# A hybrid decoder trunk on one core: the last merge on DVE, four banks for late projections, a deferred contraction block, taps behind inputs, and a shorter turn of the state space groups

## The chip, the cores and the metric

The kernel runs on one core of a Trainium2 chip. The core has a matrix engine (TensorE, PE in the profile), three engines for elementwise work (VectorE or DVE, ScalarE or ACT, GpSimd or POOL) and SyncE (SP), whose queue issues all DMAs of this kernel. The metric is device time in microseconds of one launch. Before the change it is 1704.26 us, the median of 3 runs (1700.07 to 1706.83).

## The reference

The input is one sequence of 1024 tokens of width 1024, and there are two layers. Each normalizes, mixes, normalizes the result and adds it to its input:

```python
for i in range(DEPTH):                      # DEPTH = 2
    if i % 2 == 0:
        h = rms_norm(x, attn_pre_norm)
        h = dilated_attention_mixer(h, w_in, w_out, rel_bias)
        x = x + rms_norm(h, attn_post_norm)
    else:
        h = rms_norm(x, ssm_pre_norm)
        h = s5_mixer(h, ...)
        x = x + rms_norm(h, ssm_post_norm)
```

The attention mixer projects to queries, keys and values of three groups (16 heads of 64, windows 128, 512 and 2048 with dilations 1, 4 and 16) and to a gate z. Each group gives an output and a log-sum-exp. The three outputs are merged by a softmax over the log-sum-exps, multiplied by silu(z), and projected by `w_out`:

```python
wts = softmax(stack(lses), axis=0)
o = sum(wts[..., None] * stack(outs), axis=0)
return (o * silu(z)) @ w_out
```

The state space mixer projects to u and z, runs 64 groups of 16 channels with 64 complex diagonal states over time, and gates twice:

```python
y = s5_scan(u, ...)                         # states x_t = a x_{t-1} + b u_t,  y = Re(C x) + d u
g = gelu(y)
y = g * sigmoid(g @ w_glu + b_glu)
return (y * silu(z)) @ w_out
```

## The kernel before

All matrix products take fp32 operands as a high and a low part, so each is three matmuls (high by high, high by low, low by high). Splitting a tile is a cast on ACT (L83) and a subtraction on DVE or POOL (L84), in `split`. A projection of 128 output columns is done in two halves of 512 tokens (`th` 0 and 1); a half is `proj_half`: one PSUM bank and 8 x 3 matmuls with 512 columns (L110). PSUM has eight banks, in pools of two: `psj` for projections, `pst` for transposes, `pso`, and `psl` or `psa`. The bank of a half comes free when ACT and DVE have read it.

The order of the instructions on each engine is fixed when the program is built: a planner goes by program order, by estimated times and by priorities (`high_priority(AHEAD)` moves a block ahead in program order). At run time each engine takes its instructions strictly in that order, and so does SP with its DMA issues. `issue_after(ins)` keeps the instructions of a block behind `ins` on that engine.

The stages that the change touches, in time:

1. **Attention, last pair.** Eight pairs of heads (`attn_pair`) give outputs O[0] to O[2], 128 x 1024 each, in four rotating buffers of tag `O`. `merge_weights` computes the softmax of the log-sum-exps and stores it to DRAM (`wt_dr`); `weights_of` loads it back, spread over the partitions; `merge` (L679) multiplies the three outputs by their weights and adds them up. For pairs 4 to 7 it also multiplies by the gate, which was computed early and lies in `g_dr`. The merge of pair p runs during pair p + 1 on POOL. That of the last pair (p = 7) runs at L832: products on DVE (L684, L690), the two sums on POOL (L686), with the `wraw` buffers for the weights.
2. **Gate projections** (`attn_gate`, L795). The gates of pairs 0 to 3 are projected here: eight halves through `in_order`. For each, `use` (L815) takes the silu of the bank (`silu2`: ACT L791, DVE L792), loads the pair's merged output from `on_dr`, multiplies on POOL (L822) and splits it into `gh` and `gl` (L825). `early(p)` loads and splits the finished pairs 4 to 7. The raw weights `w_out` come through `load_out` (L803).
3. **Output projection** (`attn_out`, `out_tiles`, L894). The split `w_out` (`woh`, `wol`, L938) goes to the buffers of the normalized activations (`a0` to `a3`). The first four banks, (i, n) = (0,0), (1,0), (0,1), (1,1), run over the contraction blocks k (one for each pair) at L846 to L848. With `late=0` they run over all eight before any other tile; with `late` they leave out block 7, and do it for the four banks afterwards.
4. **Layer 1** (`layer1`, L1382). Sixteen projections of two halves, eight for u and eight for z, go through `in_order` with `start="half"`, which treats the first two projections apart. After half t `run(t)` issues what the list `at` has for t: for each of eight state space groups `ssm_loads` (tables BT, Cg, Sg and CA), `ssm_taps` (eight DMAs of 64 KB, L1318), `ssm_input` (U, written by `use_u` as `u_dr`), `ssm_states` (matmuls L1339, then a chain on DVE and POOL to X) and `ssm_outputs` (matmuls L1366 and L1367, the gelu on ACT, POOL and DVE, and the store to `y_dr`). A group follows the one before by three halves. The taps of groups 0 to 3 and of 4 to 7 lie in the buffers `b1` and `b3`. `use_z` evicts a z half on ACT (L1396) and DVE (L1397).
5. **GLU** (`glu`, L1421). It loads y back (`gy`, L1431), splits it into g, whose first half (`g0b`) lies in `b1` and `b3`, and starts with four open banks, the last contraction block at the end.

The GLU's later projections and the second output projection follow, untouched.

Of the kernel before, what the change touches and what calls it, by code (L numbers as in the profile page):

```python
# [15 lines left out]
F32 = mybir.dt.float32  # L16
# [7 lines left out]
P = 128  # L24
# [89 lines left out]
def proj_half(c, w, h):  # L114

    ps = c.psj.tile([P, H], F32, tag="psj", name="psj")
    proj_part(c, ps, w, h, range(KT))
    return ps
# [504 lines left out]
def big(c, p, name):  # L623

    if p == 7:
        return c.wraw.tile([P, S], F32, tag="wraw", name=name)
    return c.attn.tile([P, S], F32, tag="mw", name=name, bufs=2)


def weights_of(c, p, g):  # L630

    w = big(c, p, "mw")
    off = c.wt_dr.offset + (p * 3 + g) * 2048
    for h in range(2):
        c.nc.sync.dma_start(w[HEADS[h]], bass.AP(c.wt_dr.tensor, off + h * S, [[0, 64], [1, S]]))
    return w


def attn_pair(c, p, w_in, h):
# [28 lines left out]
    if p == 7:  # L668
        merge_weights(c, p)
    c.merge = lambda: merge(c, p, O)  # L670
# [8 lines left out]
def merge(c, p, O):  # L679

    nc = c.nc
    for g in range(3):
        engine = nc.vector if p == 7 else nc.gpsimd
        engine.tensor_tensor(O[g], O[g], weights_of(c, p, g), op=ALU.mult)  # L684
    for g in range(2):
        nc.gpsimd.tensor_tensor(O[2], O[2], O[g], op=ALU.add)  # L686
    if p >= EARLY:
        w = big(c, p, "mg")
        nc.sync.dma_start(w, c.g_dr[p])
        (nc.vector if p == 7 else nc.gpsimd).tensor_tensor(O[2], O[2], w, op=ALU.mult)  # L690
    if p == 7:
        c.last = O[2]
    else:
        nc.sync.dma_start(c.on_dr[p], O[2])
# [54 lines left out]
def in_order(c, srcs, h, use, after=None, start=None, ws=()):  # L749
# [21 lines left out]
    elif start == "half":  # L771
        for e in range(2):
            one(e, 0, proj_half(c, ws[e], h[0]))
        pss = [c.psj.tile([P, H], F32, tag="psj", name="psj") for _ in range(2)]
        for part in range(2):
            cs = slice(part * 256, part * 256 + 256)
            for e in range(2):
                proj_part(c, pss[e][:, cs], ws[e], [x[:, :, cs] for x in h[1]], range(KT), part == 0)
                if part:
                    one(e, 1, pss[e])  # L780
    for e in range(len(ws), len(srcs)):
        w = load_w(c, srcs[e])
        for th in range(2):
            one(e, th, proj_half(c, w, h[th]))

# [9 lines left out]
def attn_gate(c, a, h):  # L795
# [9 lines left out]
    def early(p):  # L805
        load_out(p, 0)
        for i in range(2):
            if p == 7:
                f = c.last[:, i * H:i * H + H]
            else:  # L810
                f = c.slot("fz")
                nc.sync.dma_start(f, c.on_dr[p, :, i * H:i * H + H])
# [13 lines left out]

    def step(t):
        if t < 7 - EARLY:
            early(EARLY + t)

    in_order(c, [a["w_in"][48 + p] for p in range(EARLY)], h, use, step)
    run_merge(c)  # L832
# [95 lines left out]
def attn_out(c, a, g, raw):  # L928
# [28 lines left out]
    out_tiles(c, g, w, post, lambda i: xv[i], done)  # L957
# [332 lines left out]
def ssm_loads(self):  # L1290
# [8 lines left out]
    self.CA = tl("CA", 144)  # L1299
# [7 lines left out]
    nc.sync.dma_start(self.CA, c.ca_dr[et].rearrange("p (g x) -> p g x", g=8))  # L1307


def ssm_taps(self):  # L1310
# [5 lines left out]
    for m in range(8):  # L1316
        src = bass.AP(c.k_dr.tensor, c.k_dr.offset + et * 8 * 16 * 240 + 16 * m, [[240, 16], [16 * 240, 8], [1, 128]])
        c.nc.sync.dma_start(t[16 * m:16 * m + 16], src)  # L1318


def ssm_input(self):
    c = self.c
    self.U = c.ssm.tile([P, 8, P], F32, name="U", tag="U", bufs=2)
    c.nc.sync.dma_start(self.U, c.u_dr[self.et].rearrange("p (g n) -> p g n", g=8))
# [57 lines left out]
def layer1(c, a, h1, ws):  # L1382
# [20 lines left out]
    for e in range(8):  # L1403
        t = 3 * e
        for stage, d in ((ssm_loads, (-1, -2)[e] if e < 2 else 3), (ssm_taps, 4), (ssm_input, 5), (ssm_states, 7), (ssm_outputs, 10)):
            at[t + d + 1].append((stage, e))

    def run(t):
        for stage, e in at[t + 1]:
            stage(groups[e])  # L1410
# [40 lines left out]
def trunk(tc, a):  # L1451
# [3 lines left out]
    c.turn = 0  # L1455
    with ExitStack() as es:
# [160 lines left out]
```

## Time and profile before

| what | value |
|---|---|
| median of 3 runs | 1704.26 us (1700.07 to 1706.83) |
| the profiled execution | 1699.39 us |
| its span, first to last instruction | 1697.6 us |
| mean granted TensorE clock | 0.992 |
| matmuls (PE) | 9714 |
| DMA | 212.19 MB, mean 125 GB/s |
| HBM read, written | 153.51 MB, 56.96 MB |

A row of a group or of the timeline names the line of the kernel, the engine, the operation and the tiles, written before read (out<-in); x3 means three instructions. In the timeline the first two numbers are start and duration in us, and the brackets tell how long the engine sat idle before and what ended that. A row of a stretch gives its two ends and its length, then the busy time of PE, weight load (PEld), DVE, ACT and POOL, then the granted clock of TensorE as a share of full speed, the mean busy share of the DMA engines and GB/s. A row of a wait reads "who waits <- for whom: us in total, times, longest". All times in the rows count from the start of the span. SPq is SP issuing a DMA: its duration is that of the issue, not of the transfer.

### The profile page before, as it was taken

How to read it: one execution, taken by the hardware profiler on the slowest of the kernel's cores; microseconds unless marked ns; L12 is line 12 of the kernel's file. 1: busy time of each engine (PE TensorE's matmuls, PEld its weight loads, DVE VectorE, ACT ScalarE, POOL GpSimd, SP SyncE). 2: the span in 40 equal slices, each digit the busy share in tenths (PEclk: the TensorE clock that was granted, in tenths of full speed). 3: DMA queues.
4: the chain of work that ended last, by engine and by line, in shares of the span. 5: the costliest groups of instructions: out<-in, count | busy, mean ns of one | idle time of the engine just before them, and what ended most of it. 6: DMA issues, size and time to landing. Idle time of an engine off the chain costs nothing. (4 is left out here: it accounts for less than half of the span.)

```text
span 1697.6 us, 26292 instructions
## 1 busy us (share of the span) xinstructions
PE 1657.5 (98%) x9714; PEld 1397.0 (82%) x9714; DVE 1014.2 (60%) x2509; ACT 711.9 (42%) x1730; POOL 461.0 (27%) x303
## 2 busy tenths in 40 slices
PE   8999999999999999999999999999999999989998
PEld 6889999978888888888888888877887888867886
DVE  8698898625554554545454554657562787755533
ACT  5232232236465464655555454653452223233411
POOL 2000001132242525223351614213220445413121
PEclk9999999999999999999999999999999999989999
DMA  6223455532331423232242424236259865465432
GB/s 236 84 55 101 147 175 162 174 95 65 87 106 54 117 70 103 78 91 90 77 117 82 113 68 124 78 110 167 87 169 237 232 203 202 143 186 162 149 118 87
DMA packets 176857, 212.19 MB, mean 125 GB/s; under 512 B 37443, under 2 KB 133462, under 8 KB 176728
## 3 DMA queue, kind: packets, MB, share of 16 engines
q1 hardware_dynamic: 176728, 210.52, 41.5%
q8 instruction: 76, 1.25, 0.3%
q14 instruction: 53, 0.43, 0.1%
HBM read 153.51 MB, written 56.96 MB: 124 GB/s over the span
## 5 line engine op out<-in xcount | busy, mean ns | idle before, releaser
L110 PE MATMUL psj<-hh,whi 128*128 128x512 f32 x896 | 359.6, 401 | 3.7 <-DVE tz L792 3.7
L110 PE MATMUL psj<-hh,wlo 128*128 128x512 f32 x896 | 359.4, 401 | 0.0
L110 PE MATMUL psj<-hl,whi 128*128 128x512 f32 x896 | 356.4, 398 | 0.0
L84 POOL TENSOR_TENSOR wlo<-wraw,whi 128x1024 fp32r<-128x1024 f32 x48 | 115.2, 2400 | 395.4 <-ACT whi L83 365.1
L110 PEld LDWEIGHTS psj<-hh,whi 128*128 128x128 f32 x896 | 169.6, 189 | 41.2 <-DVE tz L792 4.1
L110 PEld LDWEIGHTS psj<-hh,wlo 128*128 128x128 f32 x896 | 169.4, 189 | 36.6
L110 PEld LDWEIGHTS psj<-hl,whi 128*128 128x128 f32 x896 | 169.4, 189 | 36.4
L486 ACT ACTIVATE lg<-lg,nm 128x128 f32<-128x128 f32 (+1 forms) x384 | 168.2, 442 | 37.4 <-DVE nm L481 37.4
L83 ACT CAST whi<-wraw 128x1024 fp32r<-128x1024 f32 x80 | 83.7, 1046 | 192.5 <-PE psj L110 127.1
L475 DVE CUSTOM_DVE_ANT_0 lg<-psl,T 128x128 f32<-128x128 f32 (+1 forms) x384 | 110.6, 347 | 88.6 <-PE psl L469 88.6
L371 PE MATMUL psq<-whi,v 128*128 128x256 f32 x640 | 120.3, 284 | 0.0
L110 PE MATMUL psj<-h1h,whi 128*128 128x512 f32 (+1 forms) x272 | 106.7, 393 | 8.0 <-DVE z L1397 7.8
L84 DVE TENSOR_TENSOR ph<-pt,ph 128x512 fp32r<-128x512 f32 (+2 forms) x160 | 96.8, 622 | 15.3 <-ACT ph L83 13.1
L110 PE MATMUL psj<-h1l,whi 128*128 128x512 f32 (+1 forms) x272 | 105.7, 389 | 0.1
L110 PE MATMUL psj<-h1h,wlo 128*128 128x512 f32 (+1 forms) x272 | 105.2, 388 | 0.0
L84 DVE TENSOR_TENSOR kl<-psj,kh 128x512 fp32r<-128x512 f32 x48 | 33.2, 692 | 119.8 <-ACT kh L83 119.2
L371 PEld LDWEIGHTS psq<-whi,v 128*128 128x128 f32 x640 | 100.0, 189 | 1.2 <-issue 1.2
L83 ACT CAST ph<-pt 128x512 fp32r<-128x512 f32 (+2 forms) x160 | 81.5, 529 | 46.5 <-PE pt L497 45.5
L371 PE MATMUL psq<-wlo,v 128*128 128x256 f32 x320 | 91.3, 286 | 0.5 <-DVE wlo L84 0.5
L546 PE MATMUL pso<-ph,vs 128*128 128x256 f32 (+1 forms) x544 | 86.7, 284 | 0.0
L497 PE MATMUL pt<-identr,lg 128*128 128x128 f32 x560 | 82.2, 277 | 0.0
L1213 POOL TENSOR_TENSOR Ks<-Ks,O 128x16 f32<-128x16 f32 x8 | 4.3, 534 | 284.4 <-ACT Ks L1211 284.4
(283 smaller groups left out, 3696.8 us busy)
## 6 DMA issues: line engine op xcount, KB each, us to landing
wraw<-in_w_in_dram SPq DMA_DIRECT2D x56, 512.0 KB
mw<-wt_dr SPq DMA_DIRECT2D x48, 256.0 KB
v<-in_w_v_dram SPq DMA_DIRECT2D x20, 512.0 KB
vp<-v_dr SPq DMA_DIRECT2D x16, 512.0 KB
wraw<-in_ssm_w_in_dram SPq DMA_DIRECT2D x16, 512.0 KB
v_dr<-v SPq DMA_DIRECT2D x30, 256.0 KB
rot_dr<-rt SPq DMA_DIRECT2D x48, 128.0 KB
ca_dr<-ca SPq DMA_DIRECT2D x32, 144.0 KB
```

The costliest lines, as they stand in the source:

```text
L83: nc.scalar.copy(hi, src)
L84: return (engine or nc.vector).tensor_tensor(lo, src, f32(hi), op=ALU.subtract)
L110: nc.tensor.matmul(ps, a[:, s], b[:, k, :], start=first and k == 0 and n == 0, stop=k == KT - 1 and n == 2, skip_group_check=True)
L371: nc.tensor.matmul(o, r[x][:, k, ts], w[y][:, k, :], skip_group_check=True, start=i in (0, 4, 5) and t % 2 == k == n == 0, stop=k == 3 and ...
L475: nc.vector.tensor_tensor_reduce(lg[:, h, j, 0:w], psl[:, h, o], bt[:, h, 256 - w:256], scale=1.0, scalar=-3.0e38, op0=ALU.add, op1=ALU.ma ...
L486: nc.scalar.activation(lg[:, h, j, 0:w], lg[:, h, j, 0:w], AF.Exp, bias=nm[:, h, b:b + 1], accum_out=ms[:, col:col + 1])
L497: c.nc.tensor.transpose(pt[:, n * P:(n + 1) * P], lg[:, h, j, part * P:part * P + P], c.ident)
L546: nc.tensor.matmul(o, l, r, start=n == 0, stop=n == len(jobs) - 1, skip_group_check=True)
L1213: nc.gpsimd.tensor_tensor(Ks[:, 0:16], Ks[:, 0:16], self.dd, op=ALU.add)
```

## The change

Five things change.

1. `merge` is for pairs 0 to 6 alone and runs wholly on POOL. The last pair has `merge_last`, with its two sums on DVE too. Its weights are loaded during the gate projections, after half 6, at high priority; the first goes to the fourth `O` buffer, the others to `wraw`.
2. `proj_half` takes its banks in turn from `psj` and `pst` while `c.wide` is 1: for the halves 4 to 7 of the gates, and in layer 1 from the third projection on.
3. The attention's output projection gets `late=2`: its first four banks leave out block 7 until the end.
4. In layer 1 the taps of a group are issued behind the load of its U, and CA moves from `ssm_loads` to behind them; U has three buffers instead of two. The tables of group 1 are issued behind the U of group 0.
5. Group e starts at half (11e + 2) // 4 instead of 3e: 0, 3, 6, 8, 11, 14, 17, 19. The taps come after the input instead of before it.

```diff
 def proj_half(c, w, h):
 
-    ps = c.psj.tile([P, H], F32, tag="psj", name="psj")
+    pool, tag = ((c.psj, "psj"), (c.pst, "pst"))[c.banks % 2]
+    c.banks += c.wide
+    ps = pool.tile([P, H], F32, tag=tag, name="psj")
     proj_part(c, ps, w, h, range(KT))
     return ps
...
-def big(c, p, name):
-
-    if p == 7:
-        return c.wraw.tile([P, S], F32, tag="wraw", name=name)
-    return c.attn.tile([P, S], F32, tag="mw", name=name, bufs=2)
...
 def weights_of(c, p, g):
 
-    w = big(c, p, "mw")
+    if p < 7:
+        w = c.attn.tile([P, S], F32, tag="mw", name="mw", bufs=2)
+    elif g:
+        w = c.wraw.tile([P, S], F32, tag="wraw", name="mw")
+    else:
+        w = c.outs.tile([P, S], F32, tag="O", name="mw", bufs=4)
...
     if p == 7:
         merge_weights(c, p)
+        c.last = O
     c.merge = lambda: merge(c, p, O)
...
     nc = c.nc
     for g in range(3):
-        engine = nc.vector if p == 7 else nc.gpsimd
-        engine.tensor_tensor(O[g], O[g], weights_of(c, p, g), op=ALU.mult)
+        nc.gpsimd.tensor_tensor(O[g], O[g], weights_of(c, p, g), op=ALU.mult)
     for g in range(2):
         nc.gpsimd.tensor_tensor(O[2], O[2], O[g], op=ALU.add)
     if p >= EARLY:
-        w = big(c, p, "mg")
+        w = c.attn.tile([P, S], F32, tag="mw", name="mg", bufs=2)
         nc.sync.dma_start(w, c.g_dr[p])
-        (nc.vector if p == 7 else nc.gpsimd).tensor_tensor(O[2], O[2], w, op=ALU.mult)
-    if p == 7:
-        c.last = O[2]
-    else:
-        nc.sync.dma_start(c.on_dr[p], O[2])
+        nc.gpsimd.tensor_tensor(O[2], O[2], w, op=ALU.mult)
+    nc.sync.dma_start(c.on_dr[p], O[2])
+
+
+def merge_last(c, O, w):
+
+    nc = c.nc
+    for g in range(3):
+        nc.vector.tensor_tensor(O[g], O[g], w[g], op=ALU.mult)
+        if g:
+            nc.vector.tensor_tensor(O[g], O[g], O[g - 1], op=ALU.add)
+    g7 = c.wraw.tile([P, S], F32, tag="wraw", name="mg")
+    nc.sync.dma_start(g7, c.g_dr[7])
+    nc.vector.tensor_tensor(O[2], O[2], g7, op=ALU.mult)
+    return O[2]
...
+    c.wide = 1 if start == "half" else c.wide
     for e in range(len(ws), len(srcs)):
         w = load_w(c, srcs[e])
         for th in range(2):
             one(e, th, proj_half(c, w, h[th]))
+    c.banks = c.wide = 0
...
-                f = c.last[:, i * H:i * H + H]
+                f = merged[:, i * H:i * H + H]
...
+    weights = []
+
     def step(t):
         if t < 7 - EARLY:
             early(EARLY + t)
+        c.wide = int(t >= 3)
+        if t == 2 * EARLY - 2:
+            with c.tc.high_priority(AHEAD):
+                weights.extend(weights_of(c, 7, g) for g in range(3))
 
     in_order(c, [a["w_in"][48 + p] for p in range(EARLY)], h, use, step)
-    run_merge(c)
+    c.wide = c.banks = 0
+    merged = merge_last(c, c.last, weights)
     early(7)
...
-    out_tiles(c, g, w, post, lambda i: xv[i], done)
+    out_tiles(c, g, w, post, lambda i: xv[i], done, 2)
...
     self.BT, self.Cg, self.Sg = tl("BT"), tl("Cg"), tl("Sg")
-    self.CA = tl("CA", 144)
...
-    nc.sync.dma_start(self.CA, c.ca_dr[et].rearrange("p (g x) -> p g x", g=8))
...
     t = self.M = c.taps[et // 4][:, et % 4]
-    for m in range(8):
-        src = bass.AP(c.k_dr.tensor, c.k_dr.offset + et * 8 * 16 * 240 + 16 * m, [[240, 16], [16 * 240, 8], [1, 128]])
-        c.nc.sync.dma_start(t[16 * m:16 * m + 16], src)
+    self.CA = c.ssm.tile([P, 8, 144], F32, name="CA", tag="CA", bufs=2)
+    with c.tc.issue_after(self.load_U.ins):
+        for m in range(8):
+            src = bass.AP(c.k_dr.tensor, c.k_dr.offset + et * 8 * 16 * 240 + 16 * m, [[240, 16], [16 * 240, 8], [1, 128]])
+            c.nc.sync.dma_start(t[16 * m:16 * m + 16], src)
+        c.nc.sync.dma_start(self.CA, c.ca_dr[et].rearrange("p (g x) -> p g x", g=8))
...
-    self.U = c.ssm.tile([P, 8, P], F32, name="U", tag="U", bufs=2)
-    c.nc.sync.dma_start(self.U, c.u_dr[self.et].rearrange("p (g n) -> p g n", g=8))
+    self.U = c.ssm.tile([P, 8, P], F32, name="U", tag="U", bufs=3)
+    self.load_U = c.nc.sync.dma_start(self.U, c.u_dr[self.et].rearrange("p (g n) -> p g n", g=8))
...
-        t = 3 * e
-        for stage, d in ((ssm_loads, (-1, -2)[e] if e < 2 else 3), (ssm_taps, 4), (ssm_input, 5), (ssm_states, 7), (ssm_outputs, 10)):
+        t = (11 * e + 2) // 4
+        for stage, d in ((ssm_loads, (-1, 2)[e] if e < 2 else 3), (ssm_input, 5), (ssm_taps, 6), (ssm_states, 7), (ssm_outputs, 10)):
             at[t + d + 1].append((stage, e))
...
         for stage, e in at[t + 1]:
-            stage(groups[e])
+            if stage is ssm_loads and e == 1:
+                with tc.issue_after(groups[0].load_U.ins):
+                    stage(groups[e])
+            else:
+                stage(groups[e])
```

More of the change, by code (lines that the diff above doesn't have):

```diff
@@ L1455, in trunk @@
     c.turn = 0
+    c.banks, c.wide = 0, 0
     with ExitStack() as es:
```

## The prediction

> **What bounds the kernel now.** I read the page's head first, then busy time by stretches, then what TensorE waited for, and last the order in time around each wait. TensorE has no slack to speak of:
>
> ```profile
> span 1697.6 us, 26292 instructions
> PE 1657.5 (98%) x9714; PEld 1397.0 (82%) x9714; DVE 1014.2 (60%) x2509; ACT 711.9 (42%) x1730; POOL 461.0 (27%) x303
> ```
>
> The change removes no matmul, so all that it can win is the 40.1 us in which PE is not busy and what slow clock follows. By stretches (PE busy, weight loads, DVE, ACT, POOL, granted clock, DMA):
>
> ```profile
> 0.00:1120.00 1120.00, 1110.88 (x7132) 948.12 (x7133) 675.71 (x1857) 523.47 (x1369) 293.89 (x167) 1.00 0.35 105
> 1120.00:1180.00 60.00, 52.26 (x226) 42.15 (x225) 43.47 (x64) 27.72 (x66) 18.38 (x10) 0.91 0.67 180
> 1261.00:1315.00 54.00, 51.06 (x273) 43.09 (x272) 15.77 (x46) 15.74 (x28) 2.65 (x3) 0.97 0.94 246
> 1380.00:1460.00 80.00, 75.86 (x407) 64.24 (x407) 67.34 (x95) 22.90 (x37) 40.10 (x38) 1.00 0.59 192
> 1460.00:1502.00 42.00, 38.36 (x198) 32.20 (x197) 27.66 (x39) 11.27 (x18) 12.52 (x12) 0.96 0.37 119
> 1502.00:1533.00 31.00, 26.63 (x98) 19.81 (x97) 17.46 (x24) 14.64 (x25) 7.66 (x7) 0.89 0.69 201
> ```
>
> The reader is to see that five stretches after 1120 lose time and that the clock falls in four of them. Idle time is the length less the busy time; the clock's loss I count as busy time times the missing share. A (gate projections, 1120 to 1180): 7.7 idle and 0.09 x 52.3 = 4.7 of clock. B (start of layer 1): 2.9 and 1.5. C (state space groups; two rows): 4.1 + 3.6 and 1.5. D (start of the GLU): 4.4 and 2.9. Together 22.7 + 10.6 = 33.3 us, **the most that the change can give**; the rest of the idle time lies at the start and the end, which it doesn't touch. What ended the waits from 1120 to 1540:
>
> ```profile
> PE psj L110 <- DVE z L1397: 7.8, 3, 3.6
> PE pso L848 <- DVE gl L84: 4.1, 1, 4.1
> PE psj L110 <- DVE tz L792: 3.7, 1, 3.7
> PE psb L110 <- ACT g0b L83: 3.5, 2, 2.4
> PE pv L1339 <- DMA U<-u_dr: 2.6, 1, 2.6
> ```
>
> Each edit answers to one of these.
>
> **Stretch A: four banks, merge on DVE, last block late.** My unit is the half projection (24 matmuls), from the chain:
>
> ```profile
> 1534.13 49.94 PE psj L110 x212
> ```
>
> 0.2356 us a matmul, 5.65 us a half. The rows of A in time:
>
> ```profile
> 1140.69 1.28 DVE L792 SCALAR_TENSOR_TENSOR tz<-tz,psj 128x512 f32<-128x512 f32 x2
> 1141.44 0.80 PE L110 MATMUL psj<-hh,whi 128*128 128x512 f32 x1 [3.65 <-DVE tz L792]
> 1148.60 1.23 DVE L684 TENSOR_TENSOR O<-O,mw 128x1024 f32<-128x1024 f32 x1 [2.05 <-DMA mw<-wt_dr]
> 1155.31 1.66 POOL L822 TENSOR_TENSOR fz<-fz,tz 128x512 f32<-128x512 f32 x1 [1.69 <-DMA fz<-on_dr]
> 1155.91 0.61 ACT L83 CAST woh<-wo 128x512 fp32r<-128x512 f32 x1
> 1160.79 0.86 PE L846 MATMUL pso<-woh,gh 128*128 128x512 f32 x3
> 1161.99 1.21 DVE L684 TENSOR_TENSOR O<-O,mw 128x1024 f32<-128x1024 f32 x1
> 1163.12 6.26 DVE L84 TENSOR_TENSOR wol<-wo,woh 128x512 fp32r<-128x512 f32 x3
> 1163.28 5.56 POOL L686 TENSOR_TENSOR O<-O,O 128x1024 f32<-128x1024 f32 x2 [4.24 <-DVE O L684]
> 1171.10 1.65 PE L848 MATMUL pso<-woh,gl 128*128 128x512 f32 x3 [4.09 <-DVE gl L84]
> 1171.90 6.23 DVE L84 TENSOR_TENSOR wol<-wo,woh 128x512 fp32r<-128x512 f32 x8
> 1180.53 1.28 DVE L84 TENSOR_TENSOR gl<-O,gh 128x512 fp32r<-128x512 f32 x2
> ```
>
> The sixth half waits 3.65 us for a psj bank that DVE frees late. After the change it takes a pst bank, whose last transposes belong to attention and are read out before: it starts at 1137.8 instead of 1141.4, at full clock. Three halves end at 1137.8 + 17.0 = 1154.8. The weights of the output projection are split into the places of the activations, so they follow: the first cast now comes at 1155.91, when the seventh half has read its part, and would come near 1149.5. The four open banks then take 4 x 21 matmuls without the last block, 19.8 us, to 1174.6, and 12 more, to 1177.4. Now the same 96 begin at 1160.79 and take 22.6 + 4.1 idle + about 1.4 of clock, to 1188.9. PE alone would gain 11.5.
>
> DVE must keep up. From 1148.6 it has six merge instructions (three products, two sums, the gate) at 1.23 = 7.4; 16 pieces of wol at 6.23/8 = 0.78 = 12.5; three tz at 0.64 = 1.9; five pairs of gl at about a wol piece = 3.9; the last gl 1.28. Sum 27.0, to 1175.6. That is 1 us behind where PE wants the last block: gain 10.5. What goes is the collision on lines 84 and 686: three wol pieces take 6.26 beside two POOL sums, 2.09 each against 0.78, so the two sums cost DVE 3.9 there and will cost 2.5 on it. The order is less sure: the merge stands ahead of wol in the program, and the first bank may wait for wol. I take off 1.5 for the clock after such a wait. Bounds 0 (rival 2) to 12.4 (all of A); I take **9**, nearest to the DVE sum.
>
> The weights' loads of the merge come two halves earlier, on SP, six of them, ahead of some w_out loads; the first product waits for its load now (2.05) and the third, held by a slot, ran at 1162. All three slots are separate after the change. The fourth O buffer goes to a weight, so the zero tile and the post norm's row wait for the merge to free one. The zeros are read by taps over 100 us later, and the row by the first norm, after 1177: hidden, and if the cover went, one load late, some 3 us (0 to 3, taken as 0).
>
> The Trainium skill, "SBUF — State Buffer", section "Who interferes with whom", says that a DVE instruction with two SBUF inputs and a GpSimd instruction reading SBUF exclude each other, the second waiting to the end of the first. The wol rows (2.09 beside POOL, 0.78 without) agree in kind; it also speaks against the change, because the merge on DVE now meets the L822 products. That case is rival 2.
>
> **Stretch B: taps behind inputs.**
>
> ```profile
> 1284.95 5.82 SPq L1318 DMA_DIRECT2D taps<-k_dr  x12
> 1285.85 1.06 ACT L1389 COPY ut<-psj 128x512 f32<-128x512 f32 x2
> 1291.29 5.42 SPq L1318 DMA_DIRECT2D taps<-k_dr  x11
> 1296.96 0.93 SPq L1391 DMA_DIRECT2D u_dr<-ut  x2
> 1300.76 0.98 SPq L1324 DMA_DIRECT2D U<-u_dr  x2
> ```
>
> Two ut are ready at 1286.9 and leave SP at 1297, behind 23 taps. DMA share in the stretch is 0.94. With taps of a group held behind its own U, SP has no reason to wait these 10 us; U is there before PE wants it. I take 2.6 + 1.4 = **4** (bounds 2 to 4.4). The cost: eight taps and one CA per group, nine issues at about 0.48 = 4.4 us of SP, now in each group's turn. The queue behind them holds weight loads, u, z and y stores. From 1380 the DMA share is 0.59, so I cost it at nothing; without that cover it is rival 3. CA moves past the release of its slot, and the third U buffer lets U load earlier: 0, bounds -1 to +1.
>
> **Stretch C: four banks and a shorter turn.**
>
> ```profile
> 1395.54 1.23 DVE L84 TENSOR_TENSOR wlo<-wraw,whi 128x1024 fp32r<-128x1024 f32 x1 [0.20 <-DVE T L1351]
> 1396.68 0.68 DVE L1397 SCALAR_TENSOR_TENSOR z<-z,psj 128x512 f32<-128x512 f32 x1
> 1498.72 0.38 PE L1367 MATMUL py<-X,CA 128*128 128x128 f32 x2
> 1501.62 0.39 PE L1367 MATMUL py<-X,CA 128*128 128x128 f32 x2
> ```
>
> z stands behind a group's chain on DVE. With a second pair of banks the next half needs only wlo, done at 1396.8, half a projection before it is wanted. The three waits go, with the clock's 1.5: 9.3. But the turn shrinks. A group's 48 small matmuls cost PE 48 x 2.90/26 = 5.4 (26 matmuls between the last two rows). Three halves and these are 22.3 us, 23.5 with the idle share; DVE works 67.34/80 of it, 19.8 us. The new turn is 2.75 x 5.65 + 5.4 = 20.9: DVE fits with 1.1 to spare, with less in the two turns of two halves (16.7), where it falls behind by 3 and recovers later. Outputs come three halves after states, about 17 us, which covers this. I take **8** (bounds -2 to 9.3).
>
> **Stretch D.** Outputs of the last group come two halves (11.3 us) earlier against the end of the projections.
>
> ```profile
> 1502.23 5.20 DVE L84 TENSOR_TENSOR g0b<-gy,g0b 128x512 fp32r<-128x512 f32 x6
> 1511.49 0.33 SPq L1374 DMA_DIRECT2D y_dr<-Y  x1
> 1519.27 1.22 PE L110 MATMUL psb<-g0b,whi 128*128 128x512 f32 x2 [2.40 <-ACT g0b L83]
> ```
>
> The low part of g0 lies in the taps' place, so its DVE work starts at 1502.23, right after the last py (1501.62), when PE already wants it; the last y is stored at 1511.49 and is 17.7 us behind py when PE uses it. Two halves earlier, the splits run beside PE's last projections, and the last y comes 6 us after the start, where it is wanted 19.8 us after it. The waits of 2.4 and 1.1 go, with most of the clock's 2.9; the wait for the third weight stays. I take **5** (bounds 1 to 7).
>
> **Sum.** 9 + 4 + 8 + 5 = 26 against the profiled execution of 1699.4 (span 1697.6 and 1.8 around it): 1673.4. The median shown, 1704.3, is 4.9 above that execution and the fastest run 0.7 above; I can't tell which the runs after will resemble, and forecast the middle, **1676**.
>
> One more rule is weighed because a new stall has a price beside its length. After B's wait of 2.6 us the clock (the last column but two) was:
>
> ```profile
> 1308.00:1310.00 2.00, 2.00 (x6) 1.61 (x5) 0.00 (x0) 0.00 (x0) 0.00 (x0) 0.50 1.22 194
> ```
>
> After the two of 2.1 in 1380 to 1460 it stayed 1.00. I allow 1.5, B's loss, for a new stall. The Trainium skill, "TensorE: Matmul & The Clock Gate", section "Part 1: The HAM clock gate", puts the fall behind an idle window of about 3.4 us that runs free; the wait of 2.6 is shorter and the clock fell, so length alone doesn't decide here. By length alone the new short wait would cost no clock, and A would be 10 rather than 9.
>
> **Rivals.** (1) DVE becomes the bound of the groups. For: 19.8 of 20.9, and POOL overlaps that lengthen as turns shrink. Against: DVE still waits 24.5 us for pv there.
>
> ```profile
> DVE T L1340 <- PE pv L1339: 24.5, 6, 9.1
> ```
>
> At 22 us a group it loses 1.1 x 8 = 9, and the forecast becomes 1685. (2) DVE becomes the bound of A: the merge stands ahead of wol, and five L822 of 1.66 hold it 8 us in all. A gives nothing: 1685. The page on SBUF above is its rule. (3) Slower: the spread taps delay the weight load behind them in every group. Price: the 4.4 us of SP plus 1.5 of clock, 5.9 x 8 = 47, less 26: 1676 + 47 = 1723. It decides from 3.5 us a group on, where 8 groups eat 28. Against it: a weight is loaded a whole projection ahead, and DMA is at 0.59. (4) The change doesn't do what it says: the order is fixed when the program is built, the waits move to the next weight or X, and the new orders return what the banks give: 1700, no change.
>
> **How the numbers follow.** Forecast 0.60, rival 1 0.15, rival 2 0.12, rival 4 0.08, rival 3 0.05. A measurement of this kernel can tell about 0.5% (8.5 us) from no change, so the forecast and rivals 1 and 2 are faster, 0.87; rival 4 the same, 0.08; rival 3 slower, 0.05. The low end is every loss removed, 1699.4 - 33.3 = 1666, less 2 for a good run; the high end has both DVE rivals at once, 1676 + 18 = 1694. So 1664 to 1694.
>
> **What would show it.** Right: no wait for tz L792, z L1397 or U; no POOL L686 after 1140 and single wol pieces near 0.78; U loads before the first group's taps; granted clock 1.00 from 1261 to 1502; GLU's start with one short wait. Wrong: PE waiting for wol or wo in A; py waiting for X; whi or wlo late behind taps on SP; a wait for g0b or gy at the GLU.

## The result and the profile after

The changed kernel takes 1693.5 us, the median of 4 runs (1692.35 to 1695.38), against 1704.26: a ratio of 0.9938, with an interval of 0.9925 to 0.9952. That is faster by 0.6%, and inside the range, 0.5 us under its high end. But it is a gain of 11 us where 28 were forecast. Its profiled execution took 1692.35 (span 1690.6), 7.0 under that of before. The two differ by less than the medians, because before's profiled execution is 4.9 us under its median and this one 1.2; no trace shows where these 4 us lie. One profiled execution below, that of `e1_a_only`, ran at a mean clock of 0.753 (2012.74 us) and is left out of the comparison of stretches.

First the stretches of the changed kernel, columns as before; then what PE waited for from 1120 to 1545:

```profile
1120.00:1180.00 60.00, 52.29 (x229) 41.75 (x228) 42.67 (x69) 28.38 (x66) 15.27 (x8) 0.94 0.67 189
1261.00:1315.00 54.00, 52.71 (x291) 44.75 (x290) 20.34 (x48) 16.77 (x28) 2.65 (x3) 1.00 0.71 209
1380.00:1460.00 80.00, 77.89 (x410) 66.33 (x409) 67.18 (x92) 22.22 (x36) 38.00 (x38) 0.98 0.71 204
1460.00:1502.00 42.00, 37.37 (x181) 29.28 (x181) 31.09 (x42) 16.61 (x28) 15.56 (x14) 0.94 0.51 159
1502.00:1533.00 31.00, 29.95 (x117) 23.38 (x116) 16.83 (x20) 12.82 (x20) 6.38 (x5) 0.92 0.66 199
```

```profile
PE pso L865 <- ACT gh L83: 3.9, 1, 3.9
PE pso L866 <- DVE wol L84: 3.0, 1, 3.0
PE py L1387 <- DVE X L1372: 2.1, 1, 2.1
PE psb L110 <- ACT whi L83: 1.1, 1, 1.1
PE py L1387 <- POOL Y L1391: 1.1, 1, 1.1
```

The waits of the old list for z, tz and U are gone, as forecast. Waits for gh and wol (stretch A) and for X (C) stand in their place, and at the GLU's start (D) several short ones. (Line numbers are 12 to 24 higher: L834 is the old product L822, L833 its load, L865 to L867 the output projection, L1387 py, L1394 the store of y, L1455 the load gy.)

Fixed slices mislead when the work has moved, so I also measure from one instruction to another, in us of the profiled executions. A: from the last matmul of the gates to the first of layer 1. L: from there to the first matmul of the GLU's third weight.

| profiled execution | last gate matmul | A | layer 1 begins | L | rest of the span |
|---|---|---|---|---|---|
| before | 1160.6 | 100.8 | 1261.3 | 271.5 | 164.7 |
| after | 1154.0 | 107.8 | 1261.8 | 263.2 | 165.6 |

The gates end 6.5 us earlier, and A grows by 7.0 and gives all of it back. Of these 7.0 us, 3.6 are idle time of PE (7.7 in A instead of 4.1) and 3.4 are longer busy time (100.1 instead of 96.7) for the same matmuls, at a mean clock of 0.95 instead of 0.98. The gain lies in L: 8.3. In A, the rows of PE's first wait, then of DVE, SP, POOL, ACT and PE:

```profile
1158.15 0.50 PE L866 MATMUL pso<-wol,gh 128*128 128x512 f32 x1 [3.03 <-DVE wol L84]
1156.69 6.41 DVE L84 TENSOR_TENSOR wol<-wo,woh 128x512 fp32r<-128x512 f32 x7
1163.02 0.75 DVE L84 TENSOR_TENSOR gl<-fz,gh 128x256 fp32r<-128x256 f32 x2
1163.83 1.82 SPq L833 DMA_DIRECT2D fz<-on_dr  x2
1171.29 5.03 POOL L834 TENSOR_TENSOR fz<-fz,tz 128x512 f32<-128x512 f32 x2 [11.75 <-DMA fz<-on_dr]
1174.88 0.71 ACT L83 CAST gh<-fz 128x256 fp32r<-128x256 f32 x2 [5.66 <-POOL fz L834]
1176.81 0.80 PE L865 MATMUL pso<-woh,gh 128*128 128x512 f32 x1 [3.95 <-ACT gh L83]
```

The first row is the wait for wol, whose pieces stand on DVE behind the merge. The others are read as a chain. The buffers of fz and tz come from one ring of seven slots, which later loads use again. The gl splits, behind seven pieces of wol, free slots of this ring; SP can then issue the last two fz loads. POOL multiplies 7.5 us later, when the load has landed, and PE waits 3.95 us for the cast of the product. In the kernel before, the same two loads went out five us earlier, although the gates ended 6.5 us later:

```profile
1158.82 2.46 SPq L821 DMA_DIRECT2D fz<-on_dr  x2
```

### The profile page after: what moved, and what is told of

Its sections match the earlier page's. It is cut to its first block, busy times and chain, and to the rows that moved or that the text cites. A ratio compares the mean times of both kernels' runs of the same rounds, so it can differ in the third digit from the quotient of the medians.

```text
span 1690.6 us, 26330 instructions
## 1 busy us (share of the span) xinstructions
PE 1655.9 (98%) x9714; PEld 1395.1 (83%) x9714; DVE 1012.3 (60%) x2511; ACT 712.8 (42%) x1730; POOL 452.8 (27%) x301
## 4 chain that ended last, share of the span: by engine, by line
PE 85%; DVE 7%; DMA 4%; issue 1%; POOL 1%; ACT 1%; SPq 0%; DVEq 0%; POOLq 0%; ACTq 0%
PE psj L110 45%; PE psq L373 10%; PE psl L471 5%; PE pso L548 4%; PE pt L499 4%; PE pso L865 3%; PE pso L866 3%; PE pso L867 3%; PE psb L110 1%; PE pso L574 1%; DVE T L1366 1%; DMA fz<-on_dr 1%; PE psv L234 1%; PE psv L233 1%; PE psv L232 1%
## 5 line engine op out<-in xcount | busy, mean ns | idle before, releaser
L83 ACT CAST whi<-wraw 128x1024 fp32r<-128x1024 f32 x80 | 83.7, 1046 | 161.9 <-PE psj L110 108.0
L84 DVE TENSOR_TENSOR ph<-pt,ph 128x512 fp32r<-128x512 f32 (+2 forms) x160 | 96.7, 622 | 15.3 <-ACT ph L83 13.1
L110 PE MATMUL psj<-h1l,whi 128*128 128x512 f32 (+1 forms) x272 | 104.2, 383 | 0.2 <-DVE h1l L84 0.2
```

Source lines behind the costliest of these rows:

```text
L83: nc.scalar.copy(hi, src)
L84: return (engine or nc.vector).tensor_tensor(lo, src, f32(hi), op=ALU.subtract)
L110: nc.tensor.matmul(ps, a[:, s], b[:, k, :], start=first and k == 0 and n == 0, stop=k == KT - 1 and n == 2, skip_group_check=True)
```

## The experiments

Ratios are to the kernel before, run beside each on the same chip. Kernels that stand together below ran in one set, except where a set is named.

**Which half of the change gains?** First set: `e1_a_only` has the edits of A with layer 1 as before, `e2_layer1_only` the reverse. Two more change one thing of layer 1 in the changed kernel:

```diff
# e3_turn3
-        t = (11 * e + 2) // 4
+        t = 3 * e
# e4_two_banks_l1
-    c.wide = 1 if start == "half" else c.wide
```

> The kernel before with the edits of stretch A alone (last merge on DVE, four banks for the late gate halves, last contraction block late); layer 1 as before. Theory 1: these edits move the wait instead of removing it. The gate halves end some 6.5 us earlier, then the first bank waits about 3 us for wol behind the merge and about 4 us for the last gate block, so that layer 1 starts within 1 us of before: time within 2 us of before, ratio 0.999 to 1.001. Rival: A does gain its 9 us and the changed layer 1 hands them back: 9 us faster than before, ratio 0.995 or less.

> The kernel before with the edits of layer 1 alone (taps and CA behind U, three U buffers, four banks in layer 1, shorter turn); stretch A as before. Theory 1: the whole gain of the change lies here, 7 to 10 us faster than before, ratio 0.994 to 0.996. Rival: layer 1 gives under 3 us, ratio above 0.998, because the gain was A's.

> The changed kernel with the turn of the groups back at three halves (t = 3e); all else as changed. Theory 1: the shorter turn costs a wait of py for X of 2.1 us and about 2 us of slow clock, and its earlier last y gains nothing since the gy loads are late anyway: this kernel is as fast as the changed one or up to 4 us faster. Rival: the shorter turn is what brings the GLU forward, and this kernel is 4 to 8 us slower than the changed one.

> The changed kernel with two banks instead of four in layer 1; all else as changed. Theory 1: the four banks remove the three waits for z (7.8 us and 1.5 of clock), so this kernel is 5 to 9 us slower than the changed one and shows waits for z L1397 again. Rival: DVE is the bound of the groups and the banks only defer it: within 2 us of the changed kernel.

| kernel | median us | ratio | interval | A | L |
|---|---|---|---|---|---|
| e1_a_only | 1704.42 | 1.0010 | 1.0001 to 1.0019 | | |
| e2_layer1_only | 1690.60 | 0.9929 | 0.9917 to 0.9942 | 103.4 | 262.5 |
| e3_turn3 | 1689.17 | 0.9925 | 0.9911 to 0.9938 | 107.2 | 261.8 |
| e4_two_banks_l1 | 1697.84 | 0.9975 | 0.9964 to 0.9986 | 107.1 | 270.5 |

The edits of A give nothing, those of layer 1 all. A alone needs care: `e2_layer1_only` has stretch A as before and yet an A of 103.4 against 100.8, with a wait for gl of 6.5 instead of 4.1. So a difference of up to some 3 us in A between two single traces tells nothing. Four banks are most of the gain of layer 1: without them L is 7.3 longer, and the old wait is back, larger:

```profile
PE psj L110 <- DVE z L1416: 9.0, 3, 5.3
```

The longer turn doesn't lose. In the traces it moves a loss. From the first matmul of layer 1 to the first of the GLU 227.3 us instead of 232.0, from there to the third weight 34.4 instead of 31.2, where these waits of e3_turn3 now stand:

```profile
1489.95 0.49 PE L110 MATMUL psb<-g0b,whi 128*128 128x512 f32 x1 [2.03 <-ACT whi L83]
1492.66 0.79 PE L110 MATMUL psb<-g0b,whi 128*128 128x512 f32 x1 [2.22 <-DVE g0b L84]
1508.89 0.73 PE L110 MATMUL psb<-g0b,whi 128*128 128x512 f32 x2 [2.39 <-ACT g0b L83]
```

**Second set: two guesses at the order of a queue.** In A, the last merge behind wol; at the GLU, three gy loads ahead of the last outputs, because in the changed kernel they stand behind the last y stores on SP (rows of SP, ACT and SP):

```profile
1486.74 2.87 SPq L1394 DMA_DIRECT2D y_dr<-Y  x2
1489.67 1.59 SPq L1455 DMA_DIRECT2D gy<-y_dr  x3
1493.15 0.62 ACT L83 CAST g0b<-gy 128x512 fp32r<-128x512 f32 x1 [4.13 <-DMA gy<-y_dr]
```

In the kernel before, the first three went out ten us ahead of the GLU's first matmul (1501.77); now it is four, 1489.67 against 1493.82. Its row:

```profile
1491.80 1.92 SPq L1431 DMA_DIRECT2D gy<-y_dr  x3
```

```diff
# f2b_merge_behind
-    merged = merge_last(c, c.last, weights)
-    early(7)
+    def finish(): ...          # merge_last and its two splits
...
+            with c.tc.issue_after(piece.ins):     # the last piece of wol, n = 0
+                c.finish()
# f3_gy_ahead; f23b: both, and the gates' splits at high_priority; f23bt3: with t = 3 * e
+            if stage is ssm_outputs and e == 7:
+                for et in range(3):
+                    y = c.slot("gy")
+                    nc.sync.dma_start(..., y_view(c, et, 0))
```

> The changed kernel, with the last merge put behind the seven first pieces of wol on VectorE's list. Theory (the merge stands ahead of wol there, and the late gate splits hold the fz slots): in stretch A the wait of pso for wol (3.0 us) and that for gh (3.9 us) are gone and with them a half-clock stretch; 5 to 9 us under the changed kernel, a ratio to the kernel before of 0.988 to 0.991. Rival (the last contraction block waits for whatever stands last): pso waits for the merged products instead, by as much, and the ratio stays at 0.993 to 0.995.

> The changed kernel, with the first three gy loads issued ahead of the last group's outputs. Theory (the last y stores hold the gy loads on SyncE's queue): the three gy loads go out some 10 us ahead of the block, the waits for g0b and g1b (1.2 and 0.7 us) at its start shrink and with them part of the half clock of 1496 to 1507; 2 to 5 us under the changed kernel, ratio 0.991 to 0.9925. Rival (the waits for whi and wlo, 1.1 and 0.4 us, hold the clock down by themselves): under 1 us, ratio 0.993 to 0.995.

> Both together, and the splits of the gates ranked ahead of wol's pieces. Theory (A and the GLU start are separate losses): the sum of the two, 7 to 13 us under the changed kernel, ratio 0.986 to 0.990. Rival (one gain is hidden by the other or given back in layer 1): no better than the better of the two.

> As the one before, with a turn of three steps to a state space group. Theory (the short turn makes py wait for X and half clock follow, apart from the GLU start): a further 2 to 4 us, ratio 0.984 to 0.988. Rival (the longer turn gained before only because the last y stores came behind the gy loads again): no gain over the one before, or 1 to 3 us lost, because the late groups end later.

| kernel | median us | ratio | interval | A | L |
|---|---|---|---|---|---|
| f2b_merge_behind | 1692.01 | 0.9929 | 0.9914 to 0.9944 | 108.0 | 262.0 |
| f3_gy_ahead | 1692.02 | 0.9933 | 0.9918 to 0.9948 | 108.4 | 263.4 |
| f23b | 1692.33 | 0.9931 | 0.9916 to 0.9946 | 108.9 | 261.9 |
| f23bt3 | 1691.88 | 0.9932 | 0.9916 to 0.9948 | 108.0 | 261.8 |

Both theories fell, and the two together gain no more. Three loads ahead move PE's wait to the fourth, the first behind the y stores (1494.62 in f3_gy_ahead):

```profile
1500.09 0.50 PE L110 MATMUL psb<-g0b,whi 128*128 128x512 f32 x1 [3.00 <-ACT g0b L83]
```

And f2b couldn't tell: it also put a memset of POOL between the products, and left the ring's slots as they were. In f23b the higher rank of the gates' splits didn't bring them forward: seven pieces of wol still stand ahead of them, and the last fz loads leave at 1161.83.

**Third set: what holds the last products of A?** Either VectorE and GpSimd in each other's way, or the slots.

```diff
# g1_products_dve
-        nc.gpsimd.tensor_tensor(f, f, t.rearrange(...), op=ALU.mult)
+        nc.vector.tensor_tensor(f, f, t.rearrange(...), op=ALU.mult)
# g2_spare_fz
-        f = c.slot("fz").rearrange(...)
+        f = (raw[1][:, 6 + th, :] if p == EARLY - 1 else c.slot("fz")).rearrange(...)
# g6_six_gy: as f3_gy_ahead, range(6)
```

> The changed kernel, with the gate's eight products on VectorE instead of GpSimd. Theory (in stretch A VectorE and GpSimd exclude each other, so their times add up, whatever stands first: a product takes GpSimd 1.65 us alone and 2.1 to 5.5 beside VectorE, and slows VectorE as well; on VectorE it takes about 0.65): no product of over 1 us, the waits of pso for wol and gh (3.0 and 3.9) shrink together to under 3, 3 to 6 us under the changed kernel, ratio 0.990 to 0.992. Rival (the ring's slots hold the last two fz loads until 1163): the wait for gh stays near 4 and the ratio at 0.993 to 0.995.

> The changed kernel, with the last two fz loads in a part of the second weight buffer that isn't loaded yet, so that they need no ring slot. Theory (the two engines exclude each other): the two products start earlier but run beside wol's splits, and PE waits as long elsewhere, for wol or gl; ratio 0.993 to 0.995. Rival (the slots): the loads go out some 15 us earlier, the wait for gh (3.9 us) goes with its half clock, 3 to 5 us under the changed kernel, ratio 0.990 to 0.992.

> Both: products on VectorE, and the last two without a ring slot. If the two causes are separate, 6 to 10 us under the changed kernel, ratio 0.988 to 0.990, and pso's waits under 2 us in all. If VectorE's own time is the bound of A (27 us of it after 1148, and now 4 more), no better than the better of the two alone, 0.991 to 0.995.

> The changed kernel, with six gy loads ahead of the last group's outputs (three before moved the wait to the fourth). Theory (what PE waits for at the GLU start is the first gy load that stands behind the last y stores): no wait for g0b in its first 10 us, clock back at 1.00 by 1500, 2 to 4 us under the changed kernel, ratio 0.9915 to 0.993. Rival (the ring has seven slots, and six held by gy leave the last z without one): a wait of psj for z or of psb for whi of 2 to 5 us takes its place, ratio 0.993 to 0.996.

| kernel | median us | ratio | interval | A | L |
|---|---|---|---|---|---|
| g1_products_dve | 1690.48 | 0.9924 | 0.9904 to 0.9943 | 108.0 | 263.4 |
| g2_spare_fz | 1689.31 | 0.9919 | 0.9899 to 0.9938 | 104.2 | 264.2 |
| g12 (both) | 1688.19 | 0.9910 | 0.9890 to 0.9930 | 102.6 | 262.9 |
| g6_six_gy | 1690.65 | 0.9925 | 0.9907 to 0.9943 | 106.7 | 263.0 |

The first two ratios can't be told from the changed kernel's; their traces can. With the products on VectorE the wait for gh is as long as ever, since the loads still come late (g1_products_dve, SP and PE):

```profile
1163.61 3.46 SPq L833 DMA_DIRECT2D fz<-on_dr  x2
1176.64 0.80 PE L865 MATMUL pso<-woh,gh 128*128 128x512 f32 x1 [3.97 <-ACT gh L83]
```

Without the slot they go out 11 us earlier, that wait is gone, and A is 3.6 shorter, though the second of the two products now takes 5.00 us beside VectorE's splits, and PE still waits 3.6 us for wol (g2_spare_fz, SP, POOL and PE):

```profile
1152.66 3.06 SPq L833 DMA_DIRECT2D wo<-on_dr  x2
1169.33 5.00 POOL L834 TENSOR_TENSOR wo<-wo,tz 128x512 f32<-128x512 f32 x1 [6.92 <-DVE tz L804]
1159.10 0.49 PE L866 MATMUL pso<-wol,gh 128*128 128x512 f32 x1 [3.59 <-DVE wol L84]
```

With both edits A is 102.6, and 102.9 to 103.9 in three later kernels that have them too (h1, k1 and k2), against 106.7 to 108.4 in the six with the change's own stretch A. So the slots hold the last products, and my first cause alone was the wrong one. Whether the two engines' interference costs anything beside them isn't shown: 104.2 and 102.6 are too close for single traces.

Six gy loads ahead move the wait to the seventh (2.81 us). Their five splits stand on DVE ahead of the last Y, whose stores go out at 1494.98 instead of 1486.74 (g6_six_gy, DVE and PE):

```profile
1488.39 5.97 DVE L84 TENSOR_TENSOR g0b<-gy,g0b 128x512 fp32r<-128x512 f32 x5
1494.28 1.28 DVE L1393 SCALAR_TENSOR_TENSOR Y<-Y,Y 128x512 f32<-128x512 f32 x2
1499.91 1.52 PE L110 MATMUL psb<-g0b,whi 128*128 128x512 f32 x2 [2.81 <-ACT g0b L83]
```

**Fourth set: the place of the merge, the turn, the taps**, each by itself. `h4_merge_behind_12` is g12 with the merge (and the memset of the zero tile) behind wol, `h1_12_turn3` g12 with `t = 3 * e`, `h5_merge_behind_12_turn3` both. `h3_taps_before` is the changed kernel with the old order of loads:

```diff
-        for stage, d in ((ssm_loads, (-1, 2)[e] if e < 2 else 3), (ssm_input, 5), (ssm_taps, 6), ...
+        for stage, d in ((ssm_loads, (-1, -2)[e] if e < 2 else 3), (ssm_taps, 4), (ssm_input, 5), ...
...                                   # CA back in ssm_loads, U with two buffers, no issue_after
```

> The two edits of stretch A together (products on VectorE, the last two without a ring slot), and the last merge behind wol's first eight pieces and the four gates' splits on VectorE. It differs from the kernel with the two edits in the place of the merge alone. Theory (the place of the merge costs what PE waits for wol, 2.3 us, and a stretch of half clock): wol ready when PE wants it, 2 to 4 us under the kernel with the two edits, ratio 0.9885 to 0.990. Rival (VectorE's work in A adds up to the same end whatever stands first): PE waits for gl of the last block instead, ratio 0.9905 to 0.993.

> The two edits of stretch A with a turn of three steps. Theory (the gains are in different stretches: 4.6 in A, and of the longer turn 4.7 before the GLU less 3.4 given back in it): 1 to 3 us under the kernel with the two edits, ratio 0.989 to 0.9905. Rival (the longer turn gives nothing net): 0.991 to 0.9925.

> All of these: the two edits of A, the merge behind wol, a turn of three steps. If all three add up, ratio 0.987 to 0.989; if neither the merge's place nor the turn counts, 0.990 to 0.993.

> The changed kernel, with taps, CA and U loaded as in the kernel before (taps ahead of the inputs, two U buffers). Theory (stretch B is worth 3 to 4 us by itself): PE waits for U again, about 2.6 us with some half clock, 3 to 4 us over the changed kernel, ratio 0.9955 to 0.997. Rival (the taps spread through the groups cost as much as the start gains): ratio 0.992 to 0.9945.

| kernel | median us | ratio | interval | A | L |
|---|---|---|---|---|---|
| h4_merge_behind_12 | 1692.57 | 0.9934 | 0.9922 to 0.9947 | 107.1 | 263.7 |
| h1_12_turn3 | 1685.49 | 0.9895 | 0.9881 to 0.9908 | 102.9 | 261.4 |
| h5_merge_behind_12_turn3 | 1689.66 | 0.9923 | 0.9911 to 0.9935 | 106.1 | 261.4 |
| h3_taps_before | 1688.87 | 0.9912 | 0.9898 to 0.9925 | 107.3 | 259.8 |

Of the two places tried, ahead of wol is the better one for the merge: with the long turn the intervals of h5 and h1 don't meet. Behind wol's first pieces, its three products hold up the second half's wol, for which PE then waits (h4_merge_behind_12, DVE and PE):

```profile
1166.75 3.48 DVE L698 TENSOR_TENSOR O<-O,mw 128x1024 f32<-128x1024 f32 x3
1171.55 0.80 PE L869 MATMUL pso<-wol,gh 128*128 128x512 f32 x1 [4.66 <-DVE wol L84]
```

The run with the old taps is the surprise: it is not slower than the change, and L is the shortest so far. It waits for U nowhere, and stretch B reads 52.71 busy at clock 1.00, as after:

```profile
1261.00:1315.00 54.00, 52.71 (x293) 44.76 (x292) 19.65 (x47) 17.42 (x29) 2.64 (x3) 1.00 0.95 242
1303.47 0.96 SPq L1343 DMA_DIRECT2D U<-u_dr  x2
1311.33 1.95 PE L1358 MATMUL pv<-U,BT 128*128 128x128 f32 x16
```

U leaves later than in the kernel before (1303.47 against 1300.76), but PE's list has the first pv at 1311.33, 48.8 us into layer 1; in the kernel before PE asked for it at 1306.25 - 2.62, 42.3 us into it. What the new taps cost shows at 1390, in the changed kernel (three rows of SP, two of ACT, two of DVE, one of PE):

```profile
1390.76 0.37 SPq L1394 DMA_DIRECT2D y_dr<-Y  x1
1391.76 1.78 SPq L1337 DMA_DIRECT2D taps<-k_dr  x3
1394.54 0.34 SPq L1394 DMA_DIRECT2D y_dr<-Y  x1
1396.18 0.60 ACT L1388 ACTIVATE Y<-py 128x512 f32<-128x512 f32 x1 [4.34 <-DMA y_dr<-Y]
1397.63 0.60 ACT L1388 ACTIVATE Y<-py 128x512 f32<-128x512 f32 x1 [0.36 <-DMA y_dr<-Y]
1402.60 1.10 DVE L1393 SCALAR_TENSOR_TENSOR Y<-Y,Y 128x512 f32<-128x512 f32 x1 [1.85 <-ACT Y L1392]
1414.19 1.28 DVE L1372 TENSOR_TENSOR X<-X,T 128x508 f32<-128x508 f32 x2
1414.93 0.80 PE L1387 MATMUL py<-X,CA 128*128 128x128 f32 x2 [2.11 <-DVE X L1372]
```

Four of a group's eight taps stand on SP ahead of the first y store, and seven ahead of the second. The next two Y's on ACT wait for the two buffers that these stores free, the second of them until 1397.63. Its gelu stands on DVE ahead of the scans of the next group, X comes late, and py waits 2.11 us. With the old taps (rows of h3_taps_before) both stores leave together, the second Y no longer waits (it starts at 1396.03), X is ready 1.2 us earlier, and the wait is gone:

```profile
1391.20 0.93 SPq L1393 DMA_DIRECT2D y_dr<-Y  x2
1395.06 0.60 ACT L1387 ACTIVATE Y<-py 128x512 f32<-128x512 f32 x1 [2.45 <-DMA y_dr<-Y]
1412.99 1.28 DVE L1371 TENSOR_TENSOR X<-X,T 128x508 f32<-128x508 f32 x2
```

This run puts the order of CA, the U buffers and the tables of group 1 back as well; that the cost is the taps' is read from these rows. The short turn is the other half of it: of the kernels with four banks, all ten with the short turn and the new taps show a wait of py for X, 1.9 to 3.5 us, and none of the five with the long turn does.

**Fifth set: do they add up?** g12 with the old taps, with either turn.

> The two edits of stretch A (products on VectorE, the last two without a ring slot), four banks and the short turn as changed, and taps, CA and U loaded as in the kernel before. Theory (taps in a group's turn delay the y stores on SyncE, through them X, and py waits 2.1 us with half clock behind it; A's loss is another): the two gains add, ratio 0.9875 to 0.9895, and py waits for X nowhere. Rival (the gain with the old taps was the chance of one order): as with the two edits of A alone, 0.990 to 0.992.

> The same with a turn of three steps. If the longer turn gives py its slack, the place of the taps costs nothing there: ratio as with the new taps and that turn, 0.988 to 0.991. If taps cost in any turn, 0.985 to 0.9875.

| kernel | median us | ratio | interval | A | L |
|---|---|---|---|---|---|
| k1_12_taps_before | 1684.48 | 0.9888 | 0.9871 to 0.9905 | 103.5 | 259.4 |
| k2_12_taps_before_turn3 | 1686.73 | 0.9904 | 0.9888 to 0.9921 | 103.9 | 263.3 |

k1_12_taps_before is faster than both kernels: its interval lies below that of the change, 0.9925 to 0.9952. The theory's detail was off, since py still waits 1.2 us for X, at full clock. The two times of this set can't be told apart, so for the turn I go by L in the traces. There the kernels with four banks fall into four groups: long turn and old taps 263.3 (one execution, and no other edit in layer 1), short turn and new taps 261.9 to 264.2 (ten, the change among them), long turn and new taps 261.4 to 261.8 (four), short turn and old taps 259.4 and 259.8 (two). By these the banks alone are worth 271.5 - 263.3 = 8.2 us, all that the change gains, and e4's 7.3 says nearly the same. With the short turn the new taps cost some 3.5 us (263.2 against 259.8, and 262.9 in g12 against 259.4). The rest leans on the single 263.3: the new taps alone would gain 1.7, which is less than the ten of one group differ by (2.3), the short turn alone 3.7, and both together nothing. The times of this set don't tell these two gains from nothing.

The wait for U is settled too. In k2_12_taps_before_turn3, with the old taps and the old turn, it is gone, since the first pv stands 49.9 us into the layer; in e4_two_banks_l1, with two banks, the first pv stands at 43.6, and the wait is gone because the new taps let U leave early (k2_12_taps_before_turn3, SP and PE; then e4_two_banks_l1, the same):

```profile
1299.81 0.85 SPq L1343 DMA_DIRECT2D U<-u_dr  x2
1307.73 1.95 PE L1358 MATMUL pv<-U,BT 128*128 128x128 f32 x16
```

```profile
1289.10 0.33 SPq L1343 DMA_DIRECT2D U<-u_dr  x1
1304.07 0.38 PE L1358 MATMUL pv<-U,BT 128*128 128x128 f32 x2
```

Either edit, the banks or the new taps, removes that wait; the second one gains nothing more there.

## Why the forecast was wrong

The sign was right. Of the four terms, 9 + 4 + 8 + 5, two came out at nothing, the largest among them. That the range holds the result is luck: its high end was reckoned from both DVE rivals at once, and what the runs show in the gain's place is the ring's slots, the y stores and the gy loads.

- **Stretch A, 9 forecast, -0.5 measured (layer 1 begins at 1261.8 instead of 1261.3).** The halves ended 6 us earlier, as said, and DVE's list ended at 1177.6, where the sum said 1175.6. What failed is "five pairs of gl at about a wol piece": I counted the time of these splits and not when their inputs can be there. An fz load needs a slot, the slot is freed by an earlier gl, and that gl stands behind seven pieces of wol. The last loads left SP five us later than before, and PE waited 3.95 us for them. Without the slot A is 3.6 shorter; that is the part of the miss that a run accounts for. The wait for wol that rival 2 named is there too (3.0), but another place for the merge made A no shorter (f2b) or longer (h4, h5). The clock took 3.4 us more than before, where the sum had it about even (1.4 gone, 1.5 allowed). With both edits of A (g12) layer 1 begins at 1257.2, 4.1 earlier than before, and PE still waits 5.1 us in A; what would win the rest stays open.
- **Rival 2's rule.** The Trainium skill, "SBUF — State Buffer", section "Who interferes with whom", says that a VectorE instruction with two SBUF inputs contends with a GpSimd instruction that reads SBUF. The traces agree in kind: a product took 5.00 us beside splits (g2) and 1.65 at 1143.67 of the changed kernel, and there one sum of the merge took 2.57 on VectorE beside a product and the other 1.23. Rival 2 made the two engines' work together the bound of A. But with all products off GpSimd, where the last five cost VectorE 5.6 us, A was still 108.0 and the wait for gh as long, behind loads that left late (g1).
- **Stretch B, 4 forecast, 1.6 of idle and 1.5 of clock measured.** The size was right. The reason was half of it: the taps do free U, but the banks take the same wait away by another road. Beside the banks the new taps gain nothing that can be told (1.7 by one trace), and with the short turn they lose.
- **Stretch C, 8 forecast, 5.2 measured** (240.4 - 232.0 us from the layer's start to the GLU, less B's 3.2). Four banks do what was said. With the old taps C comes to 8.8 and 7.6 (from the layer's start to the GLU 228.4 in h3 and 229.6 in k1, instead of 232.0). The step that failed is "From 1380 the DMA share is 0.59, so I cost it at nothing". DMA share isn't the cover for an issue on a queue that is worked off in order. I named the y stores behind the taps and priced only the weights, in rival 3. That rival was right in its mechanism and wrong in its place and price: one group pays, not all eight. Rival 1's wait, of py for X, came by that road, not by DVE being full: with the old taps and the same short turn it is absent in one kernel and 1.2 us in the other.
- **Stretch D, 5 forecast, -0.1 measured (31.1 us before, 31.2 after), outside its bounds of 1 to 7.** The step "the last y comes 6 us after the start" looked at the last y alone. That one came better than forecast: its store left SP by 1489.6, ahead of the GLU's first matmul at 1493.82. The earlier outputs put the last y stores ahead of all gy loads on SP, so the first y splits, which were ready before, became late. The waits of 1.06 and 2.40 turned into five of 0.23 to 1.14, with half clock.

Open: what bounds the GLU's start. Moving three or six loads, or the turn, only moved its waits. A ring with more slots was not tried.

## What to carry to other kernels

A buffer that rotates is a wait in two steps: ask which instruction frees the slot, what stands ahead of that one on its engine, and only then when the load leaves. On a queue worked off in order, price each added issue by what is behind it, above all a store that frees a buffer for the engine that feeds the critical chain. And test the parts of a change in pairs: here the new taps cost some 3.5 us only because the turn had been made shorter, and U's wait had two remedies of which one was enough.

## What the runs showed of the hardware

Half clock came without any long wait. At the GLU's start of the changed kernel no wait is over 1.14 us, and PE was busy about half the time for 8 us; the clock was then half until 1507, also when PE was busy throughout (column last but two):

```profile
1496.00:1498.00 2.00, 1.22 (x3) 0.58 (x3) 1.75 (x3) 1.30 (x3) 0.00 (x0) 0.70 0.98 294
1500.00:1502.00 2.00, 0.99 (x3) 0.50 (x2) 1.28 (x2) 1.01 (x3) 0.00 (x0) 0.50 1.04 266
1504.00:1506.00 2.00, 2.00 (x6) 1.52 (x6) 0.62 (x1) 0.00 (x0) 0.00 (x0) 0.50 1.13 336
```

The wait of 2.11 for X brought 0.50 from 1416 to 1418, that of 1.18 at the same place in k1_12_taps_before none, and two of 2.1 in the kernel before none either: the length of a wait alone didn't decide. The 1.5 us that the forecast allowed for a new stall fits the wait for X; the short ones in a row cost more, by an estimate 4 us (some 8 us of busy time at half clock, from 1496 to 1507).

A product on VectorE that reads one operand in permuted order took 1.07 to 1.19 us for 128x512, where a split of that size took 0.67 to 0.69 (g1_products_dve). The order was not tried by itself.
